# The last layer's gate and up products in seven block products instead of eight

## The chip, the cores and the metric

The kernel runs on one core of a Trainium2 chip. The metric is the device time of one execution in microseconds. Three executions of the kernel before took 2089.25, 2089.91 and 2090.18 us; the median, 2089.91 us, is what the changed kernel is held against.

## The reference

The model has two layers over 512 latent tokens (stream x) and 256 context tokens (stream c) of 1024 features. Each layer has a mixer part (pooling, windowed attention, spatial gating, three gated branches, an output projection) and then a feed-forward part. Only the feed-forward part of the second, last layer is changed:

```
def swiglu(h, w_in, w_out):
    gu = h @ w_in                                  # w_in [1024, 2 * 2816]
    return (silu(gu[..., :D_FF]) * gu[..., D_FF:]) @ w_out    # w_out [2816, 1024]

x = x + mod_x[5] * swiglu(modulate(x, norm2_gain, mod_x[3], mod_x[4]), w_ffn_in, w_ffn_out)
```

In the last layer it runs for the 512 latent tokens alone. h is the normed and modulated residual; gate is the first half of gu's columns, up is the second.

## The kernel before

**Layout.** Activations are feature-major: 128 features in the partitions, tokens along the columns; X holds the residual as 8 such tiles. A product of a weight block with the activations adds up 8 steps of 128 features in one PSUM bank.

**Split numbers.** Every large product is made of three matmuls in float32r: weights and activations are split into a high part (ScalarE copies with rounding, L272 for weights, L318 or L359 for activations) and an exact low part (VectorE subtracts, L273, L319, L360; a few on GpSimd). `gemm_step` (L289 to L292) then adds high x high, low x high and high x low. Each of these matmuls loads weights of its own.

**Weights.** `units` (L276) loads 4 KB a partition at a time from HBM into a raw tile (pool `rawp`, 4 buffers), by SyncE's queue (L284), and splits it into a `WH` and a `WL` tile (pool `hlp`, 3 buffers each). Activations, hidden tiles and the token-major result live in pool `act` (11 buffers of 8 KB a partition, tag S8).

**The feed-forward part** (`ffn`, L834). The 2816 hidden features are 22 tiles. For tile j, `half` (L873) makes the gate product of 128 features for 512 tokens (24 matmuls of 512 columns), then the up product; ScalarE takes silu of the gate out of PSUM (L883), VectorE multiplies by up (L886), and the result is split (L318, L319) into a hidden tile `fa`. After every fourth tile `chunk` (L847) makes the down products of the four tiles before: 8 feature tiles, 12 matmuls of 512 columns each, added to X by VectorE (L854). The first gate and up products of the last layer go by token halves (`first_halves`, L1036), since the second half of the tokens is normed while the first half's products run; `last_tiles` (L1015) does the same for the last output projections before it. The last two hidden tiles are multiplied with tokens in the partitions (`finish1`, L1071), into rows that `turn` (L1056) has transposed; the result is normed and stored there.

**The mixers' modulation sums.** `mod_steps` (L204) adds up weighted rows of w_mod on VectorE (L222), ScalarE and GpSimd (L220) beside the large products; its raw rows go through `rawp` too.

**What sets the order.** The lines give each instruction a priority. The framework's planner then runs the program in its own model of durations, gives each engine the ready instruction of the highest priority, and gives out tile buffers as they come free; that order is fixed in the program, and at run time each engine works through its own list and waits on semaphores.

Of the kernel before, what the change touches and what calls it, by code (L numbers as in the profile page):

```python
# [18 lines left out]
P = 128  # L19
# [16 lines left out]
class Stream:  # L36
    """Columns [t0, t0 + T) of the feature-major residual: the context or the latents."""
# [11 lines left out]
def hybrid_dit_kernel(ctx, tc, I, out):  # L49
# [4 lines left out]
    rawp = ctx.enter_context(tc.tile_pool(name="rawp", bufs=4))  # L54
    hlp = ctx.enter_context(tc.tile_pool(name="hlp", bufs=3))
# [37 lines left out]
    # rows of 128 features each, transposed to one column per row  # L93
# [50 lines left out]
    def to_features(s):  # L144
        """The stream's residual to feature-major, and its tokens' sums of squares."""
# [26 lines left out]
    def take_mod(l, t0, n, ps, nv):  # L172
        """Rows of 32 features each to columns: tiles t0 .. t0 + n of the layer's modulation vectors."""
# [11 lines left out]
    def mod_part(ps, h):  # L185
        """A quarter of the first layer's first shift and scale, on the tensor engine: loads, then two k-tiles at each step."""
# [17 lines left out]
    def mod_steps(l, u0, u1, stride=1):  # L204
        """The others, 512 at a time: weighted rows added up on the vector engines, then over the partitions."""
# [36 lines left out]
    class Filler:  # L242
        """Work that is interleaved, a step at a time, with the large products."""
# [24 lines left out]
    def split_unit(raw_ap, kt, n, nm, eng=None):  # L268
        """float32r high part and exact low part of a [P, kt, n] block of weights."""
# [6 lines left out]
    def units(src, kt, nm, engs=()):  # L276
        """src [kt*P, n] -> per n-tile (wh, wl) as [P, kt, 128] views, loaded 4 KB a partition at a time."""
# [54 lines left out]
    def token_ss(s, acc, nm):  # L332
        """Sums over the features of the squares that the tiles of acc hold."""
# [6 lines left out]
    def modulated(s, ss, A, Sh, nm, out, every=1, keep=False, HL=None):  # L340
        """Normed and modulated stream, split: the sums, the tokens' factors along the columns, the products."""
# [823 lines left out]
```

## Time and profile before

| | |
|---|---|
| median of 3 runs | 2089.91 us |
| the profiled execution, span | 2093.8 us |
| TensorE busy | 2024.5 us, 97% |
| VectorE, ScalarE, GpSimd busy | 1149.6, 744.4, 426.7 us |
| the last layer's gate, up and down products | about 1715.4 to 2073 us of the span |

The profile comes from one execution, which was 3.9 us longer than the median of the runs. Times in rows are us from the start of its span. Matmuls are pipelined: the time of one in a row overlaps the next one's, so the cost of a matmul in a long chain is the distance from one start to the next.

### The profile page before, as it was taken

How to read it: one execution, taken by the hardware profiler on the slowest of the kernel's cores; microseconds unless marked ns; L12 is line 12 of the kernel's file. 1: busy time of each engine (PE TensorE's matmuls, PEld its weight loads, DVE VectorE, ACT ScalarE, POOL GpSimd, SP SyncE). 2: the span in 40 equal slices, each digit the busy share in tenths (PEclk: the TensorE clock that was granted, in tenths of full speed). 3: DMA queues.
4: the chain of work that ended last, by engine and by line, in shares of the span. 5: the costliest groups of instructions: out<-in, count | busy, mean ns of one | idle time of the engine just before them, and what ended most of it. 6: DMA issues, size and time to landing. Idle time of an engine off the chain costs nothing.

```text
span 2093.8 us, 28850 instructions
## 1 busy us (share of the span) xinstructions
PE 2024.5 (97%) x11615; PEld 1715.0 (82%) x11615; DVE 1149.6 (55%) x1765; ACT 744.4 (36%) x1231; POOL 426.7 (20%) x358
## 2 busy tenths in 40 slices
PE   7998999999899999999999999999999999999998
PEld 6988988777677888888888888787778788888887
DVE  4878638675666653434334335765756664344335
ACT  3655434344333422121313124443422333222223
POOL 4426302023664411000102013301111130000000
PEclk9999999999999999999999999999999999999999
DMA  9755633231544232222323223423336643333331
GB/s 294 207 165 153 202 101 101 63 104 51 159 153 131 81 91 73 88 81 71 91 61 101 71 71 89 109 61 90 88 102 211 178 132 91 100 95 97 101 92 59
DMA packets 326181, 233.46 MB, mean 112 GB/s; under 512 B 7648, under 2 KB 299664, under 8 KB 326048
## 3 DMA queue, kind: packets, MB, share of 16 engines
q1 hardware_dynamic: 322528, 226.78, 36.1%
q0 software_dynamic: 3280, 4.76, 1.1%
q8 instruction: 91, 1.49, 0.3%
q14 instruction: 42, 0.34, 0.0%
q10 hardware_dynamic: 240, 0.08, 0.0%
HBM read 225.30 MB, written 2.10 MB: 109 GB/s over the span
## 4 chain that ended last, share of the span: by engine, by line
PE 81%; DVE 10%; DMA 3%; issue 2%; ACT 2%; POOL 2%; ACTq 0%; SPq 0%; POOLq 0%; DVEq 0%
PE pg1x L290 2%; PE pg1x L291 2%; PE pg1x L292 2%; PE pfg0x L292 2%; PE pfg0x L291 2%; PE pfg0x L290 2%; PE pfg1x L292 2%; PE pfo0x L290 2%; PE pfo0x L291 2%; PE pfu1x L291 2%; PE pfo0x L292 2%; PE pfu1x L292 2%; PE pfu1x L290 2%; PE pfg1x L290 2%; PE pfg1x L291 2%
## 5 line engine op out<-in xcount | busy, mean ns | idle before, releaser
L220 POOL TENSOR_TENSOR mac<-mac,mq 128x512 f32<-128x512 f32 x84 | 124.4, 1481 | 296.9 <-ACT mq L219 293.0
L273 DVE TENSOR_TENSOR wl_fu<-raw_fu,wh_fu 128x1024 fp32r<-128x1024 f32 x44 | 63.6, 1446 | 153.9 <-ACT wh_fu L272 153.8
L222 DVE SCALAR_TENSOR_TENSOR mac<-wm,scv,mac 128x512 f32<-128x512 f32 x140 | 131.0, 936 | 13.4 <-DMA wm<-in_w_mod_dram 10.6
L272 ACT ACTIVATE wh_fg<-raw_fg 128x1024 fp32r<-128x1024 f32 x44 | 46.6, 1059 | 181.1 <-PE pfo0x L292 65.7
L273 DVE TENSOR_TENSOR wl_fo<-raw_fo,wh_fo 128x1024 fp32r<-128x1024 f32 x42 | 54.7, 1303 | 69.3 <-ACT wh_fo L272 69.3
L272 ACT ACTIVATE wh_fo<-raw_fo 128x1024 fp32r<-128x1024 f32 x42 | 44.4, 1058 | 122.4 <-issue 120.2
L291 PE MATMUL pg0x<-n1x0h,wl_g0x 128*128 128x512 f32 x192 | 77.2, 402 | 8.9 <-DVE wl_g0x L273 8.9
L290 PE MATMUL pg0x<-n1x0h,wh_g0x 128*128 128x512 f32 x192 | 77.1, 402 | 1.5 <-ACT wh_g0x L272 1.5
L290 PE MATMUL pg1x<-n1x1h,wh_g1x 128*128 128x512 f32 x192 | 76.4, 398 | 0.0
L292 PE MATMUL pg0x<-n1x0l,wh_g0x 128*128 128x512 f32 x192 | 76.4, 398 | 0.0
L291 PE MATMUL pg1x<-n1x1h,wl_g1x 128*128 128x512 f32 x192 | 75.8, 395 | 0.0
L292 PE MATMUL pg1x<-n1x1l,wh_g1x 128*128 128x512 f32 x192 | 75.8, 395 | 0.0
L329 POOL TENSOR_TENSOR rs_fin<-v_fin,half_neg 128x1 f32<-128x1 f32 x4 | 2.9, 721 | 355.3 <-DVE v_fin L327 355.3
L290 PE MATMUL pfg1x<-n2x1h,wh_fg 128*128 128x512 f32 (+1 forms) x184 | 70.5, 383 | 0.8 <-ACT n2x1h L359 0.8
L854 DVE SCALAR_TENSOR_TENSOR X<-pfo0x,modv,X 128x512 f32<-128x512 f32 x48 | 36.0, 750 | 64.0 <-PE pfo0x L292 64.0
L292 PE MATMUL pfg1x<-n2x1l,wh_fg 128*128 128x512 f32 (+1 forms) x184 | 70.5, 383 | 0.5 <-POOL n2x1l L360 0.3
L290 PE MATMUL pfu1x<-n2x1h,wh_fu 128*128 128x512 f32 (+1 forms) x184 | 70.0, 380 | 0.0
L291 PE MATMUL pfu1x<-n2x1h,wl_fu 128*128 128x512 f32 (+1 forms) x184 | 70.0, 380 | 0.0
L291 PE MATMUL pfg1x<-n2x1h,wl_fg 128*128 128x512 f32 (+1 forms) x184 | 69.9, 380 | 0.0
L292 PE MATMUL pfu1x<-n2x1l,wh_fu 128*128 128x512 f32 (+1 forms) x184 | 69.9, 380 | 0.0
L290 PE MATMUL pfo0x<-fa,wh_fo 128*128 128x512 f32 x176 | 69.0, 392 | 0.0
L291 PE MATMUL pfo0x<-fa,wl_fo 128*128 128x512 f32 x176 | 69.0, 392 | 0.0
(708 smaller groups left out, 6540.1 us busy)
## 6 DMA issues: line engine op xcount, KB each, us to landing
wm<-in_w_mod_dram SPq DMA_DIRECT2D x96, 512.0 KB, 4.0
raw_fg<-in_w_ffn_in_dram SPq DMA_DIRECT2D x44, 512.0 KB, 3.9
raw_fu<-in_w_ffn_in_dram SPq DMA_DIRECT2D x44, 512.0 KB, 3.8
raw_fo<-in_w_ffn_out_dram SPq DMA_DIRECT2D x42, 512.0 KB, 3.4
raw_g0c<-in_w_in_dram SPq DMA_DIRECT2D x24, 512.0 KB, 3.9
raw_g0x<-in_w_in_dram SPq DMA_DIRECT2D x24, 512.0 KB, 4.2
raw_g1x<-in_w_in_dram SPq DMA_DIRECT2D x24, 512.0 KB, 3.9
raw_wo0c<-in_w_out_dram SPq DMA_DIRECT2D x8, 512.0 KB, 4.0
```

The lines of the kernel that those rows point to most:

```text
L220: G.tensor_tensor(a, a, q, ALU.add)
L222: V.scalar_tensor_tensor(a, raw[:, k, :], sck, a, ALU.mult, ALU.add)
L272: S.activation(wh, raw_ap, AF.Copy)
L273: (eng or V).tensor_tensor(wl, raw_ap, wh.bitcast(F32), ALU.subtract)
L290: T_.matmul(ps, wh, H, start=first, stop=False)
L291: T_.matmul(ps, wl, H, start=False, stop=False)
L292: T_.matmul(ps, wh, L, start=False, stop=last)
L329: G.tensor_tensor(rs, v, half_neg[:, :nb], ALU.pow)
L854: V.scalar_tensor_tensor(x, ps, modv[l][:, 40 + n, s.r:s.r + 1], x, ALU.mult, ALU.add)
```

## The change

The gate and up products of tile j are read as one 2 x 2 block product. The input features are halved (k tiles 0 to 3 and 4 to 7), the tokens are halved (columns 0 to 255 and 256 to 511), and the two rows of blocks are gate and up: A11, A12 are the two halves of the gate weights, A21, A22 those of the up weights; B11, B21 are the first tokens' feature halves, B12, B22 the second tokens'. Seven products of 4 k steps and 256 columns replace eight (Winograd's form of Strassen's scheme):

- weight sums on GpSimd: S1 = A21 + A22, S2 = S1 - A11, S3 = A11 - A21, S4 = A12 - S2;
- activation sums, once: T1 = B12 - B11, T2 = B22 - T1, T3 = B22 - B12, T4 = B21 - T2. B11, B21, T2, T1, T3, B22 and T4 are each split into high and low parts and kept in seven S8 tiles;
- products A11 B11, A12 B21, S2 T2, S1 T1, S3 T3, S4 B22, A22 T4. A bank P takes the products with B11, T2, T3 and T4 on top of each other, and its partial sums are read out in between; a bank R takes the ones with T1 and B22.

Each tile is four items (a: B11, B21; b: T2, T1; c: T3, B22; d: T4), each with a preparation (loads, sums, splits) and a run; down products are items too. `Pipeline` puts an item's preparation two items ahead of its run. The last layer's second norm keeps the normed tokens in float32 (`th0`, `th1`) and splits B11 and B21 as they come; `combine` makes the T's after the second token half. Tiles 0 to 2 run their item a first. `rawp` goes from 4 to 5 buffers and `hlp` from 3 to 4, for the whole kernel, and the scratch for GpSimd's DMA descriptors is set to 4096 bytes. The rows for the result and the load of final_gain are allocated at tile 21 instead of ahead of the feed-forward part. Comments are taken out.

```diff
-    rawp = ctx.enter_context(tc.tile_pool(name="rawp", bufs=4))
-    hlp = ctx.enter_context(tc.tile_pool(name="hlp", bufs=3))
+    rawp = ctx.enter_context(tc.tile_pool(name="rawp", bufs=5))
+    hlp = ctx.enter_context(tc.tile_pool(name="hlp", bufs=4))
...
+    class Pipeline:
+        def fill(self):
+            while len(self.ready) <= self.depth:
+                item = next(self.items, None)
+                if item is None:
+                    return
+                self.ready.append((item[1], item[0]()))
+        def step(self):
+            self.fill()
+            if not self.ready:
+                return False
+            do, w = self.ready.popleft()
+            do(w)
+            fill.tick()
+            return True
...
+        def split(self, nm, src, k0, k1, eng):
+            c = self.C[nm]
+            S.activation(c[:, 0, k0:k1, :], src, AF.Copy)
+            eng.tensor_tensor(c[:, 1, k0:k1, :], src, c[:, 0, k0:k1, :].bitcast(F32), ALU.subtract)
...
+        def norm(self, st, ss, i):
...
+            for k in range(KT):
+                V.tensor_tensor(t[:, k, :], X[:, k, st.cols], rb, ALU.mult)
+                a, b = A2[l][:, k, st.r:st.r + 1], modv[l][:, 24 + k, st.r:st.r + 1]
+                if k % 2:
+                    S.activation(t[:, k, :], t[:, k, :], AF.Identity, bias=b, scale=a)
+                else:
+                    V.tensor_scalar(t[:, k, :], t[:, k, :], a, b, ALU.mult, ALU.add)
+                if i == 0 and k % 2:
+                    nm = "B11" if k < 4 else "B21"
...
+                    self.split(nm, t[:, k - 1:k + 1, :], (k - 1) % 4, (k - 1) % 4 + 2, G if k % 4 == 1 else V)
+        def combine(self):
...
+            for h in (slice(0, 2), slice(2, 4)):
+                V.tensor_tensor(b11[:, h], b12[:, h], b11[:, h], ALU.subtract)
+                V.tensor_tensor(T2[:, h], b22[:, h], b11[:, h], ALU.subtract)
+                self.split("T2", T2[:, h], h.start, h.stop, V)
+            self.split("T1", b11, 0, 4, G)
+            V.tensor_tensor(b12, b22, b12, ALU.subtract)
+            self.split("T3", b12, 0, 4, V)
+            self.split("B22", b22, 0, 4, G)
+            V.tensor_tensor(b21, b21, T2, ALU.subtract)
+            self.split("T4", b21, 0, 4, V)
+        def product(self, ps, w, k0, nm, first):
+            c = self.C[nm]
+            wh, wl = w
+            for k in range(4):
+                H, L = c[:, 0, k, :], c[:, 1, k, :]
+                T_.matmul(ps, wh[:, k0 + k, :], H, start=first and k == 0, stop=False, skip_group_check=True)
+                T_.matmul(ps, wl[:, k0 + k, :], H, start=False, stop=False, skip_group_check=True)
+                T_.matmul(ps, wh[:, k0 + k, :], L, start=False, stop=k == 3, skip_group_check=True)
...
+            def sums():
...
+                s1, s2, s3, s4 = (att.tile([P, 4, P], F32, tag="pr", bufs=4, name=f"S{x}{j}") for x in (1, 2, 3, 4))
+                G.tensor_tensor(s1, a21, a22, ALU.add)
+                G.tensor_tensor(s2, s1, a11, ALU.subtract)
+                G.tensor_tensor(s3, a11, a21, ALU.subtract)
+                G.tensor_tensor(s4, a12, s2, ALU.subtract)
...
+            def run_a(w):
+                d["P"] = ps_y.tile(...)[:, :256] if early == "y" else pmain(f"pP{j}")[:, :256]
+                self.product(d["P"], w, 0, "B11", True)
+                S.activation(d["m"][:, 0:256], d["P"], AF.Copy)
+                ps = pmain(f"pS{j}")[:, :256]
+                self.product(ps, w, 4, "B21", True)
+                V.tensor_tensor(d["g_"][:, 0:256], ps, d["m"][:, 0:256], ALU.add)
+                S.activation(d["g_"][:, 0:256], d["g_"][:, 0:256], AF.Silu)
+            def run_b(w):
+                self.product(d["P"], w, 0, "T2", False)
+                S.activation(d["m"][:, 256:512], d["P"], AF.Copy)
+                d["R"] = pmain(f"pR{j}")[:, :256]
+                self.product(d["R"], w, 4, "T1", True)
+                S.activation(d["m5"], d["R"], AF.Copy)
+            def run_c(w):
+                self.product(d["P"], w, 0, "T3", False)
+                V.tensor_tensor(d["h"][:, 256:512], d["P"], d["m5"], ALU.add)
+                self.product(d["R"], w, 4, "B22", False)
+                V.tensor_tensor(d["g_"][:, 256:512], d["R"], d["m"][:, 256:512], ALU.add)
+                S.activation(d["g_"][:, 256:512], d["g_"][:, 256:512], AF.Silu)
+            def run_d(w):
+                self.product(d["P"], w, 0, "T4", False)
+                V.tensor_tensor(d["h"][:, 0:256], d["P"], d["g_"][:, 0:256], ALU.mult)
+                G.tensor_tensor(d["h"][:, 256:512], d["h"][:, 256:512], d["g_"][:, 256:512], ALU.mult)
+                split_act(*A(), d["h"])
...
-    mixer(SX, 1, *hs["x"], ..., mid=context_keys, last=last_tiles)
-    ffn([SX], 1, hs, finish1, parts=first_halves, ahead=..., turn=turn)
+    tail.extend(ffn_seven(seven, SX, 1, finish1, turn_out))
+    mixer(SX, 1, *hs["x"], ..., mid=context_keys, last=last_tiles)
+    run(norms[1])
+    seven.combine()
+    tail[1]()
...
-    nc = bacc.Bacc("TRN2", target_bir_lowering=False, num_devices=1)
+    nc = bacc.Bacc("TRN2", target_bir_lowering=False, num_devices=1, dynamic_dma_scratch_size=4096)
```

The weights' preparation of a tile splits 1024 columns for item a (A11, A12), 512 each for S2, S1, S3 and S4, and 512 for A22. `ffn_seven` holds the down products of four tiles as four items of two feature tiles each, as before after every fourth tile, into banks of pool `ps_s`.

## Rows read from the trace of the kernel before

**Rows 1.** Page, part 1: engine, busy us, share of the span, instructions.

```profile
PE 2024.5 (97%) x11615; PEld 1715.0 (82%) x11615; DVE 1149.6 (55%) x1765; ACT 744.4 (36%) x1231; POOL 426.7 (20%) x358
```

**Rows 2.** Page, part 4: the chain that ended last, share by engine.

```profile
PE 81%; DVE 10%; DMA 3%; issue 2%; ACT 2%; POOL 2%; ACTq 0%; SPq 0%; POOLq 0%; DVEq 0%
```

**Rows 3.** Busy time by stretch; the first line names the columns.

```profile
core 0: us, PE busy (x) PEld busy (x) DVE busy (x) ACT busy (x) POOL busy (x), PEclk, DMA share, GB/s
...
110.00:235.00 125.00, 116.44 (x964) 111.53 (x963) 97.99 (x154) 67.02 (x117) 57.45 (x52) 0.99 0.59 174
...
345.00:500.00 155.00, 152.03 (x954) 119.85 (x952) 107.19 (x235) 70.22 (x150) 30.88 (x32) 1.00 0.27 77
500.00:660.00 160.00, 143.25 (x695) 112.52 (x695) 102.71 (x107) 59.66 (x84) 91.22 (x56) 0.95 0.46 139
...
1500.00:1660.00 160.00, 159.21 (x812) 126.61 (x812) 100.67 (x154) 50.22 (x76) 28.72 (x24) 1.00 0.49 151
...
1715.40:1732.50 17.10, 15.77 (x125) 14.30 (x124) 13.89 (x35) 13.14 (x28) 7.72 (x10) 1.00 0.32 93
1732.50:2073.00 340.50, 340.49 (x1517) 282.10 (x1516) 137.35 (x149) 90.27 (x109) 0.00 (x0) 1.00 0.31 92
```

**Rows 4.** PE timeline (start us, us): two starts 24 matmuls apart, for each width.

```profile
1702.06 0.28 PE L292 MATMUL po1x<-yo1x,wh_wo1x 128*128 128x256 f32 x1
...
1704.94 0.28 PE L292 MATMUL po1x<-yo1x,wh_wo1x 128*128 128x256 f32 x1
...
1803.23 0.39 PE L290 MATMUL pfu1x<-n2x1h,wh_fu 128*128 128x512 f32 x1
...
1808.67 0.39 PE L290 MATMUL pfg1x<-n2x1h,wh_fg 128*128 128x512 f32 x1
```

**Rows 5.** Groups by line, DVE, 1732.5 to 2073: busy us, mean ns, idle before.

```profile
L854 DVE SCALAR_TENSOR_TENSOR X<-pfo1x,modv,X 128x512 f32<-128x512 f32 x40 | 30.0, 750 | 44.1 <-PE pfo1x L292 44.1
...
L273 DVE TENSOR_TENSOR wl_fg<-raw_fg,wh_fg 128x1024 fp32r<-128x1024 f32 x20 | 24.5, 1225 | 7.4 <-ACT wh_fg L272 7.4
...
L319 DVE TENSOR_TENSOR fa<-sg1x,fa 128x512 fp32r<-128x512 f32 x21 | 14.4, 685 | 0.0
```

**Rows 6.** Groups by line, ACT, from 1690 on.

```profile
L272 ACT ACTIVATE wh_fg<-raw_fg 128x1024 fp32r<-128x1024 f32 x22 | 23.3, 1060 | 78.9 <-PE pfo1x L292 39.4 <-issue 19.6 <-PE pfu1x L292 19.4
...
L318 ACT ACTIVATE fa<-sg1x 128x512 fp32r<-128x512 f32 x22 | 13.5, 616 | 2.4 <-DVE sg1x L886 2.4
...
L359 ACT ACTIVATE n2x1h<-t_n2x 128x256 fp32r<-128x256 f32 x16 | 6.3, 412 | 2.3 <-DVE t_n2x L358 2.0
```

**Rows 7.** Groups by line, POOL, whole span.

```profile
L372 POOL TENSOR_TENSOR sq_m1x<-sq_m1x,sq_m1x 128x512 f32<-128x512 f32 x4 | 7.1, 1763 | 21.8 <-ACT sq_m1x L368 21.8
...
L717 POOL TENSOR_TENSOR ws0x<-a0x 128x527 f32<-128x527 f32 x4 | 4.3, 1066 | 36.6 <-issue 21.9 <-ACT a0x L711 14.7
```

**Rows 8.** Groups by line, DVE: 1715 to 1732.5, then the whole span.

```profile
L354 DVE TENSOR_TENSOR t_n2x<-X,ps_rb_n2x 128x256 f32<-128x256 f32 x15 | 5.7, 408 | 1.0 <-PE ps_rb_n2x L346 1.0
...
L273 DVE TENSOR_TENSOR wl_g0x<-raw_g0x,wh_g0x 128x1024 fp32r<-128x1024 f32 x24 | 38.1, 1586 | 37.4 <-ACT wh_g0x L272 37.3
```

**Rows 9.** Timeline at the start of the feed-forward part.

```profile
1715.88 0.39 PE L290 MATMUL pfg1x<-n2x1h,wh_fg 128*128 128x256 f32 x1
...
1723.88 0.75 DVE L354 TENSOR_TENSOR t_n2x<-X,ps_rb_n2x 128x256 f32<-128x256 f32 x2 [0.99 <-PE ps_rb_n2x L346]
...
1730.62 0.53 DVE L360 TENSOR_TENSOR n2x1l<-t_n2x,n2x1h 128x256 fp32r<-128x256 f32 x1 [0.48 <-ACT n2x1h L359]
```

**Rows 10.** What PE waited for, whole span: us in total, times, longest.

```profile
PE pg0x L291 <- DVE wl_g0x L273: 8.9, 3, 4.8
...
PE pb0x L291 <- DVE wl_b0x L273: 5.6, 2, 4.7
```

**Rows 11.** The longest such wait's end: SP's load, and PE's stretch after.

```profile
550.64 0.37 SPq L284 DMA_DIRECT2D raw_g0x<-in_w_in_dram  x1
...
562.00:566.00 4.00, 3.90 (x9) 3.13 (x10) 0.65 (x2) 0.00 (x0) 3.69 (x3) 0.50 0.67 207
```

More of the change, by code (lines that the diff above doesn't have):

```diff
@@ L1 @@
 import math
+from collections import deque
 from contextlib import ExitStack
@@ L941, in ffn, with __init__ @@
         chunk(heads[-1])
+    class Pipeline:
+        def __init__(self, items, depth):
+            self.items, self.depth, self.ready = iter(items), depth, deque()
+        def fill(self):
[12 more added lines that the diff above has]
+            return True
@@ L1011, in hybrid_dit_kernel @@
     norms = []
-    us_first = []
-    ahead = up_units(1, 0, FCH * P)
+    seven = Seven(1)
+    tail = []
     def last_tiles(one, acc):
-        hs["x"] = pair_tiles(KT, SEQ, "n2x1")
         for i, st in enumerate(halves):
@@ L1020, in last_tiles @@
             part = [acc[0][:, c]]
-            norms.append(modulated(st, partial(token_ss, st, part, f"n2x1{i}"), A2[1], modv[1][:, 24:32, :], f"n2x1{i}", [],
-                                   HL=[[y[:, c] for y in x] for x in hs["x"]]))
+            norms.append(seven.norm(st, partial(token_ss, st, part, f"n2x1{i}"), i))
             for n in range(KT - 3, KT):
@@ L1026, in last_tiles, with turn_out @@
                 if i and n == KT - 3:
[L1027 removed]
+                    steps(norms[0], 1)
                 elif i and n == KT - 2:
+                    steps(norms[0], 2)
+                    tail[0].fill()
+                elif i:
                     steps(norms[0], 1)
[L1030 to L1033 removed]
         run(norms[0])
[L1036 to L1053 removed]
+    late = {}
     ssf = cst.tile([P, 4, 2], F32, name="ssf")
[L1056 removed]
+    def turn_out(i):
         if i == 0:
+            late["yt"] = [act.tile([P, 2, D], F32, tag="S8", name=f"yt{x}") for x in range(2)]
+            rows = act.tile([P, 2, D], F32, tag="S8", name="rows")
+            fg, mrow = late["rows"] = rows[:, 0, :], rows[:, 1, :]
+            nc.gpsimd.dma_start(fg, I["final_gain"].unsqueeze(0).to_broadcast([P, D]))
             ps = ps_s.tile([P, 1024], F32, tag="ps", name="ps_mrow")
@@ L1062, in turn @@
             S.activation(mrow, ps, AF.Copy)
+        yt = late["yt"]
         for b in range(2):
@@ L1073, in finish1 @@
         ws = []
+        yt = late["yt"]
+        fg, mrow = late["rows"]
         for c in range(2):
@@ L1116, in finish1 @@
         store(3)
-    ffn([SX], 1, hs, finish1, parts=first_halves, ahead=[chain([w], us) for w, us in zip(us_first, ahead)], turn=turn)
+    tail.extend(ffn_seven(seven, SX, 1, finish1, turn_out))
+    mixer(SX, 1, *hs["x"], mods=mod_steps(1, 4, 10), end=lambda: fill.add(mod_steps(1, 10, 12)), mid=context_keys, last=last_tiles)
+    run(norms[1])
+    seven.combine()
+    tail[1]()
 _INS = ["x", "c", "ctx", "c_ctx", "w_mod", "b_mod", "norm1_gain", "norm2_gain", "w_in", "w_pool", "pool_scale",
```

142 lines of the change are left out of this document (121 added, 21 removed).

## The prediction

> **What bounds the kernel now.** I read the page's busy shares first, then the chain, then the busy times by stretch, then the starts of single matmuls. TensorE is busy 97% of the span, VectorE 55% [rows 1], and the chain that ended last lies on PE for 81% and on DVE for 10% [rows 2]. The stretches say where that holds: from 1732.5 to 2073, where the last layer's gate, up and down products run, PE is busy 340.49 of 340.5 us while DVE is busy 137 and ACT 90 and POOL nothing [rows 3]. There nothing but the number and width of the matmuls sets the time. It does not hold everywhere: from 500 to 660 PE loses 16.75 of 160 us, and from 1715.4 to 1732.5, the entry of the changed part, it is short of inputs too [rows 3]. So the change has four places to be priced: the products themselves, their entry, the new load on the other engines beside them, and, because two buffer pools grow for the whole kernel, the mixers ahead of them.
>
> **The products.** In the chain, 24 matmuls of 512 columns take 1808.67 - 1803.23 = 5.44 us, 0.2267 each, and 24 of 256 columns 1704.94 - 1702.06 = 2.88 us, 0.120 each [rows 4]. Half the columns is thus not half the time: 2 x 0.120 is 0.0133 us above 0.2267. Both rows have new weights for each matmul, so the price of loading weights twice as often per column is in them.
> Before, a tile takes 48 matmuls of 512 columns, 10.88 us; the first tile goes by token halves, 96 of 256, 11.52 us. All 22: 21 x 10.88 + 11.52 = 240.0 us. After, a tile takes 7 products x 4 steps x 3 = 84 matmuls of 256 columns, 10.08 us; all 22: 221.8 us. The change removes 18.2 us of TensorE time: 12.5% of the columns, but 7.6% of the time.
> The Trainium skill ("TensorE: Matmul & The Clock Gate", Back-to-back issue gap) gives a matmul N columns over 2.4 GHz plus about 2.5 ns, so 0.216 and 0.109 us. By that the tile would go from 10.36 to 9.17 us and the saving would be some 26 us; the two rows are 0.011 us above it at either width, and since there are more matmuls after than before, that difference speaks against the change. The rows decide.
>
> **The entry.** T2 can't be made before the second token half is normed, while item a needs the first half alone. Before, the factors of the second half reach DVE at 1723.88 and its last low part is cut at 1730.62, with PE waiting in between [rows 9]. From 1715.4 to 1732.5 PE had 96 x 0.120 = 11.5 us of product and some 2 us of small matmuls (norm sums, factors, w_mod sums), so about 3.6 of 17.1 us were lost. After, counted from the same 1723.88: DVE has 8 multiplications by the factors (0.408 each [rows 8]) and 4 scalings of the same width (taken as 0.408), 4.9 us; then, at 512 columns and 0.685 each [rows 5], two subtractions for T1, two for T2 and two low parts of T2, 4.1 us, with one ACT copy of 0.616 [rows 6] not covered. T2 is ready near 1733.5. Items a of tiles 0 to 2 need only B11 and B21; they are 72 x 0.120 = 8.6 us from 1715.88 on, with the small matmuls and the read-outs between their second products until about 1726.5. So PE runs dry for some 7 us. Then DVE still has T3, T4, their low parts (4 x 1.225 [rows 5]) and the low weights of items c and d of tile 0 (3 x 0.685): T4's product of tile 0 ends near 1742, by when PE has done 17.3 us of products and 2 us of small work of 26.5. The loss is about 7.5 us for 3.6 before: 4 us more. And a gap of that length costs more behind it: after PE's wait that ended at 562, the granted clock is 0.50 for 562 to 566, the level of 1.2 GHz [rows 11]; some 5 us at half speed are worth about 2.5 us. I take 6 us for the entry. Lower bound 0, if the planner fills the gap with later items' first products; upper bound 11, if DVE runs beside POOL at the rate of rows 8 (1586 against 1225 ns [rows 5], so 14 us of DVE work become 18).
>
> **The other engines beside the products.** For a tile with its share of down products PE now has 10.08 + 5.44 = 15.5 us. DVE: 1.225 + 5 x 0.685 for the low weights, 0.685 for the low hidden tile, 1.225 for the low down weights, 2 x 0.750 for X [rows 5], and four read-outs of 256 columns at 0.408 [rows 8]: 9.7 us, 62%, where it was 40% [rows 3]. ACT: 2 x 1.060, 6 x 0.616, five read-outs or silus at 0.412 [rows 6]: 7.9 us, 51%. POOL, idle before: 4 sums of 512 columns, 1.07 us each when undisturbed and 1.76 when not [rows 7], and one product of 256: 5 to 8 us, 32 to 50%. SP's queue has the same loads. No engine passes PE, so by load the cover holds. What is new is that PE itself waits: bank P is read out three times within a tile, each time behind a product of 1.44 us into another bank, which must cover a semaphore, an ACT or DVE queue that may be inside an operation of 1.06 to 1.23 us, and the read-out of 0.41. The planner has other work to put there (down products, the next tile's item a), but by its own durations. The trace has no such stage; the nearest ones by load are four [rows 3]: 1500 to 1660 (DVE 63%, ACT 31%, POOL 18%), where PE is idle 0.5%; 345 to 500 (69, 45, 20), 1.9%; 110 to 235 (78, 54, 46), 6.8%; 500 to 660 (64, 37, 57), 10.5%. I take 345 to 500, nearest in DVE and ACT: 2% of 331 us (221.8 + 5 x 96 x 0.2267) is 6.5 us. Bounds: 1.7 and 35 us.
>
> **The end.** Behind the last tile's d stand a multiplication of 256 columns, a copy and a subtraction of 512, 0.41 + 0.62 + 0.69 us. Before, the rows' transposes covered the same chain; now they come one item earlier, but the final products of the hidden tile before (9 matmuls of 512 columns in three banks, 2.0 us) need only that one. Cost 0; if that cover is gone, 2 us.
>
> **The mixers.** One more raw tile and one more pair of split tiles let a load and a split run one unit further ahead. From 500 to 660 PE's waits for low weights are 8.9 and 5.6 us [rows 10]; for the longest, the raw weights were asked for only at 550.64 and PE resumed at 562 at half clock [rows 11]. The granted clock of 0.95 over those 160 us [rows 3] is another 8 us. All of it together is 22 us, the most to be had. But the low weights also queue behind w_mod sums on DVE, and the planner's new order may open waits of its own; the trace bounds that loss by nothing, and I allow 5 us. I take a gain of 8 us, a bit over a third. The smaller scratch for GpSimd's descriptors is shown by no row; its few transfers in the mixers may wait a little, 0 to 3 us, taken as 0.
>
> **The sum.** -18.2 + 6 + 6.5 - 8 = -13.7 us. On the profiled execution's 2093.8 us that is 2080.1; its span stands 3.9 us above the median of the runs, so 2076 in runs.
>
> **The rivals.**
> 1. The buffers matter more than the products: the waits from 500 to 660 go, and the planner covers the read-outs as from 1500 to 1660: -18.2 + 6 + 1.7 - 22 = -32.5, so 2057. For it: the late load in rows 11. Against it: the DVE queue.
> 2. The gain is eaten: entry 11, read-outs 3% (10 us), mixers unchanged: +3, so 2086 to 2094 with small differences. For it: every one of PE's new waits has a cover of only 1.44 us.
> 3. Slower: DVE and POOL disturb each other through the whole stretch, run behind the planner's order, and PE waits as from 500 to 660, 10.5%: -18.2 + 6 + 35 - 5 = +18, so 2108. It decides from 7% of idle PE on (24 us). For it: POOL goes from 0 to 32 to 50% here, and both engines' rows are half again as long in company [rows 5, 7, 8]. Against it: 1500 to 1660, with the same DVE load, and that the waits from 500 to 660 stand behind long runs of w_mod sums, which this stretch has none of. The Trainium skill ("SBUF — State Buffer", Who interferes with whom) calls the port that the two share an exclusive lock; if each subtraction and each sum waited its turn, that would be this rival.
> 4. That the products get no shorter, since loading weights might set the pace at 256 columns: excluded by the 0.120 us of rows 4.
>
> **Chances.** Forecast 0.57, rival 1 0.14, rival 2 0.14, rival 3 0.15. About 0.2%, 4.2 us, is what a measurement can tell: faster is below 2085.7, slower above 2094.1. The forecast and rival 1 lie below: faster 0.71, same 0.14, slower 0.15. The range 2058 to 2096 leaves out most of rival 3 and half of rival 1.
>
> **What would show it.** Starts 0.120 us apart in the seven products; 84 of them a tile; a gap of some 7 us in PE near 1726 with half clock behind it; PE's idle share from there to the end near 2%, with waits on the read-outs; DVE near 62% and POOL near 40%; in the mixers fewer waits for low weights. The prediction is wrong if PE's idle share there is above 5%, if the entry costs nothing, or if the mixers move by more than 15 us.

## The result, and the profile after

The changed kernel took 2145.24 us in the median of four runs (2140.53 to 2148.37), the kernel before 2090.05 in the same session: a ratio of 1.0259, 95% interval 1.0242 to 1.0276. It is 55 us slower, where 14 us faster was forecast, and it lies above the whole range.

The page's busy times by engine, after (as [rows 1]):

```profile
PE 2031.1 (95%) x12359; PEld 1751.9 (82%) x12359; DVE 1264.9 (59%) x1923; ACT 807.9 (38%) x1401; POOL 591.6 (28%) x464
```

The busy times by stretch: first those of [rows 3], then the entry (up to the first down product) and the rest of the last feed-forward part.

```profile
core 0: us, PE busy (x) PEld busy (x) DVE busy (x) ACT busy (x) POOL busy (x), PEclk, DMA share, GB/s
110.00:235.00 125.00, 112.62 (x905) 106.21 (x905) 93.12 (x153) 64.75 (x119) 55.32 (x49) 0.96 0.53 159
345.00:500.00 155.00, 153.39 (x937) 122.36 (x936) 112.23 (x234) 72.06 (x150) 30.14 (x32) 1.00 0.28 80
500.00:660.00 160.00, 149.16 (x767) 117.17 (x766) 108.75 (x122) 63.30 (x96) 96.49 (x60) 0.97 0.47 141
1500.00:1660.00 160.00, 156.43 (x817) 123.59 (x816) 93.25 (x146) 49.66 (x76) 30.96 (x26) 1.00 0.46 142
1726.10:1800.40 74.30, 60.07 (x431) 57.24 (x429) 61.28 (x86) 40.04 (x74) 41.21 (x25) 0.86 0.24 72
1800.40:2127.00 326.60, 302.08 (x1970) 275.28 (x1969) 207.53 (x255) 128.67 (x230) 123.38 (x87) 0.96 0.28 83
```

Before, the last stretch of [rows 3] had PE busy 340.49 of 340.5 us at clock 1.00 and POOL empty. Now PE idles 14.2 of the entry's 74.3 us and 24.5 of the next 326.6, at clocks of 0.86 and 0.96, with POOL busy 38% beside it. The products themselves are as short as forecast: in the timeline of TensorE (start, us), two starts 24 matmuls apart are 1840.49 - 1837.62 = 2.87 us, 0.120 each, as in [rows 4].

```profile
1837.62 0.28 PE L1038 MATMUL pP<-cbT,wh_su 128*128 128x256 f32 x1
...
1840.49 0.28 PE L1038 MATMUL pS<-cbB,wh_sg 128*128 128x256 f32 x1
```

To say where the 52.8 us between the two profiled executions (2093.8 and 2146.6) lie, I took the distance from each matmul's start to the next, took off 0.120 or 0.2267 us, and called what is left over lost: waits, half-clock matmuls, small matmuls between. The marks are the end of the last output projection (po1x), the first down product (pfo1x) and the first of the final products.

| part | before | after | difference |
|---|---|---|---|
| up to the last po1x | 1715.4 | 1726.1 | +10.7 |
| pure products of the last feed-forward part | 348.6 | 330.1 | -18.5 |
| lost in its entry | 5.5 | 25.4 | +19.9 |
| lost from there to the final products | 4.8 | 45.1 | +40.3 |
| the whole of that part, mark to mark | 359.2 | 401.0 | +41.8 |
| behind it | 19.2 | 19.5 | +0.3 |

(The parts of the feed-forward part fall 0.3 to 0.4 us short of the marks, at the stretches' edges. Of the 4.8 and 45.1 us, 4.4 and 5.1 are the transposes of the result's rows ahead of the final products.) What TensorE waited for from 1726 on, after (us in total, times, longest):

```profile
PE pfo1x L291 <- DVE X L1146: 17.7, 5, 4.1
PE pP L1038 <- ACT m L1104: 10.9, 11, 2.6
PE pP L1038 <- ACT cbT L984: 4.8, 1, 4.8
PE pP L1039 <- DVE wl_sc L1070: 2.7, 1, 2.7
```

The first comes back at every chunk of down products; the second is the read-out of bank P, 3 times in the entry and 8 times behind it, between the chunks (6.8 us there). One wait of the first kind, in the timeline of all engines (loads of weights and the matmuls between left out):

```profile
1871.06 1.29 POOL L1057 TENSOR_TENSOR S<-raw_u 128x512 f32<-128x512 f32 x1 [8.58 <-DVE gt L1115]
...
1871.67 1.77 DVE L274 TENSOR_TENSOR wl_fo<-raw_fo,wh_fo 128x1024 fp32r<-128x1024 f32 x1 [0.72 <-ACT wh_fo L273]
...
1872.43 2.16 POOL L1058 TENSOR_TENSOR S<-S,raw_g 128x512 f32<-128x512 f32 x1
...
1873.69 1.98 DVE L274 TENSOR_TENSOR wl_fo<-raw_fo,wh_fo 128x1024 fp32r<-128x1024 f32 x1
1874.56 2.27 POOL L1059 TENSOR_TENSOR S<-raw_g,raw_u 128x512 f32<-128x512 f32 x1
1876.79 1.28 POOL L1060 TENSOR_TENSOR S<-raw_g,S 128x512 f32<-128x512 f32 x1
...
1878.03 0.72 POOL L1121 TENSOR_TENSOR h<-h,gt 128x256 f32<-128x256 f32 x1
1878.78 0.63 ACT L319 ACTIVATE fa<-h 128x512 fp32r<-128x512 f32 x1 [5.31 <-POOL h L1121]
...
1879.44 0.69 DVE L320 TENSOR_TENSOR fa<-h,fa 128x512 fp32r<-128x512 f32 x1 [3.77 <-ACT fa L319]
1880.05 1.40 DVE L1146 SCALAR_TENSOR_TENSOR X<-pfo1x,modv,X 128x512 f32<-128x512 f32 x2
1880.94 0.77 PE L291 MATMUL pfo1x<-fa,wh_fo 128*128 128x512 f32 x1 [3.38 <-DVE X L1146]
1881.50 0.63 PE L292 MATMUL pfo1x<-fa,wl_fo 128*128 128x512 f32 x1
```

Read it backwards. PE waits 3.38 us for a bank that X's update (L1146) must empty. VectorE does X late, because its list has the low part of the hidden tile (L320) ahead of it; that waits for ScalarE's copy, and that for the h product on GpSimd (L1121), which stands behind the next tile's four weight sums. The sums themselves take 1.28 to 2.27 us; the VectorE subtraction of 1024 columns beside them takes 1.77 and 1.98 us, 1.225 before [rows 5]. By these rows the two engines take turns: the sum that starts at 1872.43 ends 1.15 us after the end of the subtraction beside it (1871.67 + 1.77 = 1873.44), the next subtraction ends 1.08 us after the end of that sum (1874.59), the next sum 1.16 us after that subtraction's (1875.67). Each thus lasts about its own time behind the other's end. It is the same over the whole stretch from 1800.4 on: when the rest of the other engine's running operation is taken off, the 66 VectorE subtractions that overlap a GpSimd operation take 0.54 to 0.69 us (512 columns) or 1.08 to 1.23 (1024), where undisturbed ones take 0.68 to 0.69 and 1.21 to 1.23. Behind the gap the matmuls are 0.43 us apart: from 1881 to 1886 the granted clock is 0.50, the level of 1.2 GHz, after the wait of 3.38 us. So two causes are mixed here, a queue (h behind the sums) and a mutual slowing of GpSimd and VectorE. And a third place, the pools, moved the mixers. The experiments take them apart.

### The profile page after: what moved, and what is told of

Read it like the earlier page. It is cut to its first block, busy times and chain, and to the rows that moved or that the text cites. A ratio compares the mean times of both kernels' runs of the same rounds, so it can differ in the third digit from the quotient of the medians.

```text
span 2146.6 us, 30872 instructions
## 1 busy us (share of the span) xinstructions
PE 2031.1 (95%) x12359; PEld 1751.9 (82%) x12359; DVE 1264.9 (59%) x1923; ACT 807.9 (38%) x1401; POOL 591.6 (28%) x464
## 5 line engine op out<-in xcount | busy, mean ns | idle before, releaser
L291 PE MATMUL pfo1x<-fa,wh_fo 128*128 128x512 f32 x160 | 67.1, 419 | 17.7 <-DVE X L1146 17.7
L274 DVE TENSOR_TENSOR wl_fg<-raw_fg,wh_fg 128x1024 fp32r<-128x1024 f32 x22 | 34.5, 1567 | 64.4 <-ACT wh_fg L273 64.3
L1057 POOL TENSOR_TENSOR S<-raw_u 128x512 f32<-128x512 f32 x22 | 32.0, 1453 | 142.6 <-DVE wl_sb L1070 97.9
L291 PE MATMUL pfg0x<-n2x0h,wh_fg 128*128 128x512 f32 x176 | 68.9, 391 | 0.4 <-ACT n2x0h L360 0.4
L293 PE MATMUL pfg0x<-n2x0l,wh_fg 128*128 128x512 f32 x176 | 68.9, 391 | 0.2 <-DVE n2x0l L361 0.2
L291 PE MATMUL pfo0x<-fa,wh_fo 128*128 128x512 f32 x176 | 69.0, 392 | 0.0
L292 PE MATMUL pfg0x<-n2x0h,wl_fg 128*128 128x512 f32 x176 | 68.7, 391 | 0.0
L293 PE MATMUL pfo0x<-fa,wh_fo 128*128 128x512 f32 x176 | 68.6, 390 | 0.0
L291 PE MATMUL pfu0x<-n2x0h,wh_fu 128*128 128x512 f32 x176 | 68.5, 389 | 0.0
L292 PE MATMUL pfu0x<-n2x0h,wl_fu 128*128 128x512 f32 x176 | 68.5, 389 | 0.0
L293 PE MATMUL pfu0x<-n2x0l,wh_fu 128*128 128x512 f32 x176 | 68.5, 389 | 0.0
```

What stands on the lines that cost most here:

```text
L274: (eng or V).tensor_tensor(wl, raw_ap, wh.bitcast(F32), ALU.subtract)
L291: T_.matmul(ps, wh, H, start=first, stop=False)
L292: T_.matmul(ps, wl, H, start=False, stop=False)
L293: T_.matmul(ps, wh, L, start=False, stop=last)
L1057: G.tensor_tensor(s1, a21, a22, ALU.add)
```

## The experiments

Each was timed against the kernel before, which had a median of 2089.95 to 2091.35 us in the sessions.

**The pools alone, in the kernel before.**

```diff
-    rawp = ctx.enter_context(tc.tile_pool(name="rawp", bufs=4))
-    hlp = ctx.enter_context(tc.tile_pool(name="hlp", bufs=3))
+    rawp = ctx.enter_context(tc.tile_pool(name="rawp", bufs=5))
+    hlp = ctx.enter_context(tc.tile_pool(name="hlp", bufs=4))
...
-    nc = bacc.Bacc("TRN2", target_bir_lowering=False, num_devices=1)
+    nc = bacc.Bacc("TRN2", target_bir_lowering=False, num_devices=1, dynamic_dma_scratch_size=4096)
```

> The kernel before with the pool sizes of the change alone (five raw tiles, four pairs of split tiles, the smaller scratch). Up to the start of the last feed-forward part the changed kernel is 10.8 us later than the one before (last output projection at 1726.3 for 1715.5). Theory A, the pools reorder the mixers and that costs: about 2101 us, with PE's waits on score read-outs near 90 to 135 and on tanh read-outs in the gates. Theory B, the mixers are later because the planner works around the new part: 2090 us, no change. My prediction's own term, the pools help by 8: 2082 us.

2098.75 us, ratio 1.0039 (1.0024 to 1.0054). The pools cost, where I had them gain 8 us. What TensorE waited for over the span of this run:

```profile
PE pt0c L536 <- DVE pr0c L522: 7.3, 4, 4.4
...
PE s1x L505 <- ACT pr1x L518: 3.1, 1, 3.1
...
PE pg0x L291 <- DVE wl_g0x L273: 0.2, 1, 0.2
```

The wait for low weights of [rows 10], 8.9 us, is gone, as forecast. But the context's attention now waits 7.3 us for VectorE's normalised probabilities, 2.4 before, and the context's mixer ends 10 us later (261.3 to 271.4). The changed kernel shows the same two lines, 7.2 and 0.4 us. These two nearly cancel: the last down product of layer 0's latent tokens ends at 1258.2 us here, at 1260.8 before and at 1258.6 in the run with the smaller descriptor space alone (below). What is left of the loss is in layer 1's mixer, 459.5 us long here for 454.5 before, where one wait in the attention (s1x) grew from 0.2 to 3.1 us.

**The h product on VectorE.**

```diff
-                G.tensor_tensor(d["h"][:, 256:512], d["h"][:, 256:512], d["g_"][:, 256:512], ALU.mult)
+                V.tensor_tensor(d["h"][:, 256:512], d["h"][:, 256:512], d["g_"][:, 256:512], ALU.mult)
```

> The changed kernel with one line moved: the product of silu(gate) and up for the second 256 tokens on VectorE instead of GpSimd. Theory Q (queues): that product stands behind four weight sums on GpSimd, the hidden tile's split behind it, the updates of X behind that on VectorE, both banks of the down products stay full and PE waits 3.4 us and falls to half clock, five times: 18 us of waits and 9 us of clock go, about 2120 us. Theory P (VectorE and GpSimd slow each other by the shared port, whatever the order): the waits move elsewhere, 2140 us or more.

2129.58 us, ratio 1.0187 (1.0170 to 1.0203): 16 us back, by taking the product out of GpSimd's queue. The loss behind the entry falls from 45.1 to 30.8 us; the rest stays.

**Both banks of each ps_s tile for the down products.**

```diff
+                    pair = ps_s.tile([P, 1024], F32, tag="ps", name=f"pfo{l}{s.name}{c0}{n}")
                     for i in range(2):
-                        ps = ps_s.tile([P, 1024], F32, tag="ps", name=f"pfo{l}{s.name}{c0}{n + i}")[:, :512]
+                        ps = pair[:, i * 512:(i + 1) * 512]
```

> The changed kernel with both banks of each down-product tile used: four banks for the down products instead of two, nothing else. Theory Q: PE may run four feature tiles ahead of VectorE, 10.9 us instead of 5.4, so a delay of 3.4 us is covered: the 18 us of waits and the 9 us of clock behind them go, about 2120 us. Theory P: VectorE is late for good, the waits come back within the chunk: 2140 us or more.

2149.82 us, ratio 1.0284 (1.0269 to 1.0300). No gain, and the wait on X grows:

```profile
PE pfo1x L291 <- DVE X L1147: 23.9, 5, 5.3
```

By the code a pair of banks is freed only when both its feature tiles are added to X, which may be why the wait grew; no run takes that apart. What is late is VectorE, not the number of banks; the queue theory's forecast for this run fell.

**No weight sums.**

```diff
-                G.tensor_tensor(s1, a21, a22, ALU.add)
-                G.tensor_tensor(s2, s1, a11, ALU.subtract)
-                G.tensor_tensor(s3, a11, a21, ALU.subtract)
-                G.tensor_tensor(s4, a12, s2, ALU.subtract)
-                d["S"] = s1, s2, s3, s4
+                d["S"] = a21, a22, a11, a12
```

> The changed kernel without the four weight sums on GpSimd: the blocks themselves are split in their place, so the output is not the reference's. Theory Q: GpSimd's queue is empty, the product for the second tokens comes at once: as with that line moved, about 2115 us, and the start of the part gains some 5 us as its factors no longer wait behind sums, 2110 us. Theory P: VectorE runs undisturbed too, all of the stretch's 30 us of waits and 10 us of clock go and most of the start's loss: below 2100 us.

2097.47 us, ratio 1.0036 (1.0024 to 1.0049): 48 us less than the change. Behind the entry 6.4 us are lost of 45.1, and 5.1 of those are the rows' transposes. The profile shows no wait of TensorE there at all. So nearly the whole loss hangs on the four sums; the 84 matmuls, the read-outs of bank P and the seven combinations cost TensorE some 1.3 us there, and the h product, which is on GpSimd in this run too, costs nothing without the sums ahead of it.

**The sums and the product on VectorE, with the large and with the old pools.**

```diff
-                G.tensor_tensor(s1, a21, a22, ALU.add)
-                G.tensor_tensor(s2, s1, a11, ALU.subtract)
...
+                V.tensor_tensor(s1, a21, a22, ALU.add)
+                V.tensor_tensor(s2, s1, a11, ALU.subtract)
...
```

> The four weight sums (L1057 to L1060) and the h product (L1121) move from GpSimd to VectorE; nothing is left out. VectorE has then some 4 x 0.69 + 0.41 = 3.2 us more per tile of 14.8 us, and no two-input work of GpSimd beside it. Theory G (what hurts is GpSimd: its sums slow VectorE's parts, and the product queues behind them): the steady part comes back to within 5 us of the run without sums, 2097 to 2108 us. Rival L (the work itself is too much, wherever it is done: VectorE at some 85 % becomes late for the residual update and for the low parts): 2120 us or more, with TensorE waits on VectorE in every tile.

> As the run before it, with the old pools besides (rawp 4, hlp 3, the default descriptor space). Theory A (the larger pools cost the mixers 8 us, as in the kernel before with larger pools, and the sevens need none of them): 6 to 10 us below the run with the large pools. Rival B (the sevens need the fourth weight buffer, since each product now has half the columns and a weight pair lasts 10 us / 3.5): the gain in the mixers is paid back in the last layer, the same time within 3 us or more, with TensorE waits on weight parts in the steady part.

2100.14 us (ratio 1.0045, 1.0031 to 1.0060) and 2099.77 (1.0041, 1.0026 to 1.0056). The same work on the engine that is the busier one costs TensorE next to nothing behind the entry: the stretch 1800 to 2040 has PE busy 239.62 of 240 us with VectorE at 74% and GpSimd empty. Theory L fell. (The low parts of T1 and B22, in the entry, are still GpSimd's in both runs.)

```profile
1800.00:2040.00 240.00, 239.62 (x1680) 224.97 (x1679) 177.83 (x291) 111.81 (x203) 0.59 (x1) 1.00 0.34 101
```

With the old pools the mixers end 7.7 us earlier (1715.1 for 1722.8), the feed-forward part takes 5.7 longer (362.7 for 357.0), 4.8 of it in the entry, and the end behind it 2.0 longer (21.6 for 19.6): rival B in effect, though its place is the entry and not the steady part.

**Operations of GpSimd that nobody waits for.** First as copies of the sums without loads to wait for, with the h product on VectorE and on GpSimd:

```diff
+                va, vb = vtm[:, 0:4, :], vtm[:, 2:6, :]
-                G.tensor_tensor(s1, a21, a22, ALU.add)
+                G.tensor_tensor(s1, va, vb, ALU.add)
...
-                d["S"] = s1, s2, s3, s4
+                d["S"] = a21, a22, a11, a12
```

> Four GpSimd operations of the same kind and size per tile, but on tiles that nobody waits for; the weight blocks are used without sums (so what is computed is not the scheme's result), and the h product is on VectorE. What is left of GpSimd is only its presence beside VectorE. Theory P (sharing slows VectorE's parts from 0.69 to 1.4 to 1.8 us, and that makes the residual updates late): near the run with only the h product moved, 2115 to 2132 us. Theory Q (only who waits for GpSimd matters: the weight parts for the sums, the h product behind them): 2095 to 2101 us, as without sums.

> As the run before it, the h product on GpSimd again, so that it stands in GpSimd's queue behind the four operations. Theory Q: the queue gives back most of the loss, 2110 to 2125 us, while the run before it is at 2098. Theory P: the run before it has most of the loss and this one 10 to 18 us more, as the h product was worth in the changed kernel (2145 against 2130).

2153.74 and 2150.84 us (ratios 1.0303, 1.0286 to 1.0321, and 1.0286, 1.0271 to 1.0302). They answer another question than I put. The planner drew all 88 operations forward into layer 1's mixer, where their operand was ready from 1526 on, and the last layer ran without them (355.5 and 354.9 us). Two stretches of that mixer in the first of the two runs:

```profile
1560.00:1620.00 60.00, 46.95 (x210) 37.09 (x208) 50.20 (x37) 9.47 (x11) 59.30 (x36) 0.93 0.50 151
1620.00:1680.00 60.00, 36.90 (x128) 28.37 (x129) 22.98 (x21) 7.75 (x10) 51.84 (x39) 0.73 0.26 76
```

GpSimd is full, the mixer's own GpSimd operations stand behind the copies, and PE loses 36 of 120 us. For theories P and Q they are void; in the next run the operations are tied to the loads.

```diff
                 G.tensor_tensor(s4, a12, s2, ALU.subtract)
-                d["S"] = s1, s2, s3, s4
+                d["S"] = a21, a22, a11, a12
...
-                G.tensor_tensor(d["h"][:, 256:512], d["h"][:, 256:512], d["g_"][:, 256:512], ALU.mult)
+                V.tensor_tensor(d["h"][:, 256:512], d["h"][:, 256:512], d["g_"][:, 256:512], ALU.mult)
```

> The two runs with sums of other tiles had them in the wrong place: the planner drew operations without loads to wait for forward into the mixer. Here the four weight sums are made by GpSimd of the loaded blocks, as in the change, but nobody reads them (the parts are made of the weight blocks themselves, so what is computed is not the scheme's result), and the h product is on VectorE. Theory P (GpSimd beside VectorE slows VectorE's parts and updates, and that alone makes TensorE wait): near the run with only the h product moved, 2115 to 2132 us, with TensorE waits on VectorE. Theory Q (the loss comes by those that wait for the sums): as without sums, 2095 to 2101 us.

2128.52 us, ratio 1.0176 (1.0161 to 1.0191). Nobody reads a sum, and 31 of the 48 us are there: theory P. By the marks of the table above, 21 of the 31 lie behind the entry, 3 in it and 7 ahead of it; there the first tiles' sums also stand ahead of a small step of the norm in GpSimd's queue, for which TensorE waits 2.9 us. The groups of VectorE from 1840 to 2060 (busy us, mean ns, idle before) tell how, first in the change, then in this run, then with the sums on VectorE:

```profile
L1070 DVE TENSOR_TENSOR wl_sc<-S,wh_sc 128x512 fp32r<-128x512 f32 x26 | 26.0, 1011 | 1.4 <-ACT wh_sc L1069 1.0
...
L274 DVE TENSOR_TENSOR wl_fo<-raw_fo,wh_fo 128x1024 fp32r<-128x1024 f32 x12 | 18.7, 1559 | 9.7 <-ACT wh_fo L273 9.7
L1146 DVE SCALAR_TENSOR_TENSOR X<-pfo1x,modv,X 128x512 f32<-128x512 f32 x24 | 17.7, 749 | 31.7 <-PE pfo1x L293 31.7
L320 DVE TENSOR_TENSOR fa<-h,fa 128x512 fp32r<-128x512 f32 x13 | 16.6, 1275 | 11.3 <-ACT fa L319 11.3
L1070 DVE TENSOR_TENSOR wl_su<-raw_u,wh_su 128x512 fp32r<-128x512 f32 x13 | 16.5, 1272 | 0.0
```

```profile
L274 DVE TENSOR_TENSOR wl_fo<-raw_fo,wh_fo 128x1024 fp32r<-128x1024 f32 x12 | 19.1, 1595 | 9.7 <-ACT wh_fo L273 9.7
L1146 DVE SCALAR_TENSOR_TENSOR X<-pfo1x,modv,X 128x512 f32<-128x512 f32 x24 | 17.7, 747 | 27.2 <-PE pfo1x L293 27.2
L320 DVE TENSOR_TENSOR fa<-h,fa 128x512 fp32r<-128x512 f32 x14 | 12.8, 913 | 0.0
```

```profile
L1146 DVE SCALAR_TENSOR_TENSOR X<-pfo1x,modv,X 128x512 f32<-128x512 f32 x30 | 22.5, 749 | 20.6 <-PE pfo1x L293 20.6
L274 DVE TENSOR_TENSOR wl_fo<-raw_fo,wh_fo 128x1024 fp32r<-128x1024 f32 x16 | 19.5, 1221 | 10.1 <-ACT wh_fo L273 10.1
...
L320 DVE TENSOR_TENSOR fa<-h,fa 128x512 fp32r<-128x512 f32 x14 | 9.6, 684 | 0.0
```

With both inputs in SBUF an operation stretches from 684 to 913 or 1275 ns, from 1221 to 1559 or 1595. X's update, which has one input in PSUM, takes 749, 747 and 749: it does not stretch, nor do the 8 of its 40 operations that overlap one of GpSimd's in the changed kernel (0.75 us each). So the loss behind the entry splits by the runs' traces: 20.8 us by the mutual slowing (27.2 lost with unread sums and h on VectorE, less 6.4 without sums), 3.6 by the parts that wait for the sums (30.8 with the sums read, h on VectorE), and 14.3 by the h product's place behind the sums (45.1). The place, since the same product on GpSimd without sums costs nothing (6.4 us lost); the steps are differences between runs whose order the planner may have changed elsewhere too.

**Another entry: tiles 0 and 1 as eight products.** Gate and up of tiles 0 and 1 go by token halves with B11, B21, then B12, B22; the T's are made meanwhile on VectorE, T2, T1, T3 and T4 behind the four `then` items.

```diff
+            yield g0, lambda w: h0("g", 0)
+            yield u0, lambda w: h0("u", 0)
+            yield g1, lambda w: h1("g", 0)
+            yield lambda: None, then(h0, ("g", 1))
+            yield lambda: None, then(h0, ("u", 1))
+            yield lambda: None, then(h1, ("g", 1))
+            yield u1, then(h1, ("u", 0), ("u", 1))
+            for j in range(2, NF):
```

> Sums and h product on VectorE, old pools, and another entry: hidden tiles 0 and 1 go as eight plain products by token halves, which need no second half and no T; the T's are made beside them, on VectorE, and tiles 2 to 21 go as seven. The sevens then save 20/22 of 18.6 us = 16.9. The run with old pools lost 24 us at the entry (72.7 us for 48.8 of products); theory N (what was missing is work for TensorE that needs no T): some 5 us of loss stay, 2099.8 - 19 + 1.7 = 2082 us, 2077 to 2087. Rival S (VectorE with some 11 us of sums and parts, or the 11 tiles of 8 KB, are late all the same): the loss moves to the first product with T2, 2090 us or more.

> As the run before it with the larger pools (rawp 5, hlp 4, descriptor space 4096). The mixers end some 7.7 us later with them; with the small pools the entry of the sevens was 5 us longer, which the plain tiles no longer need. Theory A: 5 to 9 us above the run with the old pools. Rival B (the fourth weight buffer is needed at the plain tiles too, whose parts are held for both halves): the same within 3 us.

2082.04 us with the old pools, ratio 0.9955 (0.9938 to 0.9971): faster than both kernels, at theory N's number. The entry loses 7.3 us (59.0 for 51.7 of products), 23.9 with the T's in the way (72.7 for 48.8). Two things changed in it, the plain tiles and the low parts of T1 and B22, which left GpSimd; no run tells the two apart. From 17 us into the entry on, the stretch 1726.1 to 1800 has PE busy 73.37 of 73.9 us, at clock 1.00:

```profile
1726.10:1800.00 73.90, 73.37 (x520) 68.78 (x519) 59.42 (x89) 37.34 (x62) 0.00 (x0) 1.00 0.32 93
```

With the large pools 2090.35 us, 0.9995 (0.9985 to 1.0004): 8 us more, theory A.

**Which of the pools.** The first line below alone, then with the second, then with the third.

```diff
+    nc = bacc.Bacc("TRN2", target_bir_lowering=False, num_devices=1, dynamic_dma_scratch_size=4096)
...
+    rawp = ctx.enter_context(tc.tile_pool(name="rawp", bufs=5))
...
+    hlp = ctx.enter_context(tc.tile_pool(name="hlp", bufs=4))
```

> The kernel before with the descriptor space of 4096 alone, pools as they were. With larger pools and this space it took 2098.75. Theory D (the space is what costs, by GpSimd's transfers): 2096 to 2100 us. Theory A (the buffers are what costs, by another order of the planner): 2088 to 2092 us.

> The kernel before with the descriptor space of 4096 and rawp at 5 buffers; hlp stays at 3. Both larger pools together took 2098.75 us, the space alone 2090.56. Theory R (a fifth raw buffer lets the sums of w_mod and later loads run further ahead and shares the transfers otherwise, which delays the first mixer's weights): 2096 to 2100 us. Theory H (not this one): 2088 to 2092 us.

> The kernel before with the descriptor space of 4096 and hlp at 4 buffers; rawp stays at 4. Theory H (a fourth weight buffer lets ScalarE and VectorE split weights earlier than what the mixer itself waits for, which costs more than it gives): 2096 to 2100 us. Theory R: 2088 to 2092 us, or less, since low weights are what the mixers wait for most.

The space alone: 2090.56 us (0.9999, 0.9989 to 1.0008). The fifth raw buffer: 2075.70 (0.9930, 0.9915 to 0.9945). The fourth weight buffer: 2092.47 (1.0004, 0.9994 to 1.0013). Neither costs anything measurable alone; theories R and H both fell. The raw buffer alone gives 15 us: the wait of [rows 10] for pg0x's low weights shrinks from 8.9 to 1.2 us, and the context's attention does not pay for it (mixer's end at 262.4 us, 261.3 before).

```profile
PE pb0x L291 <- DVE wl_b0x L273: 4.3, 2, 3.5
...
PE pg0x L291 <- DVE wl_g0x L273: 1.2, 1, 1.2
```

The fourth weight buffer alone brings part of the attention's waits (4.6 us, the context's mixer's end at 265.8), both together 7.3 us. The longer mixer of layer 1 comes with both only: 459.5 us, with the raw buffer alone 451.1, with the weight buffer alone 453.0, with the descriptor space alone 452.9. That the planner lets splits of weights go ahead of the softmax on VectorE is my reading and was not taken apart.

**All that helped.** The plain entry, sums and product on VectorE, hlp 3, and five or six raw buffers.

> The sevens with plain tiles 0 and 1, sums and h product on VectorE (2082.04 us with the old pools), now with the fifth raw buffer and the 4096 descriptor space, hlp at 3. Theory R (the fifth raw buffer frees the latent mixer of layer 0 of its waits for low weights, whatever the last layer does): the kernel before gained 15 us by it, so 2067 us, 2063 to 2071. Rival O (the planner's order of the mixers depends on all that follows, and the gain belongs to that one program): 2078 us or more.

> As the run before it with six raw buffers. Theory R2 (one more removes the waits that five leave: 4.3 us at the third branch's low weights in layer 0's latent mixer): 2 to 5 us below five. Rival F (five are enough, and a sixth only lets later loads go ahead of earlier needs): the same or up to 8 us more.

2069.51 us (0.9896, 0.9881 to 0.9910) and 2067.52 (0.9889, 0.9871 to 0.9907): the raw buffer's gain carries over, 12.5 of 15 us. A sixth is 2 us better in the median, with runs that overlap; it is not settled. The feed-forward part takes 348.9 us with five, 359.2 before, and behind its entry TensorE is full:

```profile
1756.70:2046.00 289.30, 289.29 (x1967) 268.22 (x1966) 214.68 (x340) 129.43 (x230) 0.59 (x1) 1.00 0.32 95
```

Seven products are worth 6 us here against the kernel before with the raw buffer alone (2075.70, in another session), where the feed-forward part alone gained 10 (348.9 for 359.2); the rest went into mixers that end later (1698.6 for 1694.6).

## Why the prediction was wrong

**The products: right.** -18.2 forecast, -18.5 found, at 0.120 and 0.2267 us apiece. By the spacing that the Trainium skill ("TensorE: Matmul & The Clock Gate", Back-to-back issue gap) gives for a matmul by itself, the saving would have been an estimated 26 us; the trace is with the rows.

**The other engines beside the products: this step failed, and it decides.** It read "The trace has no such stage; the nearest ones by load are four" and "I take 345 to 500, nearest in DVE and ACT: 2% of 331 us ... is 6.5 us". The runs found 40.3. The loads were forecast well (VectorE 62%, found 60% undisturbed, 172.51 of 288 us in the run without sums, and with the waiting for GpSimd 207.53 of 326.6, 64%; GpSimd about 40%, found 38%). So was what the term was named for: without the sums, that stretch loses 1.6 us more than in the kernel before (6.4 for 4.8). The choice of the stage was wrong: 345 to 500 has POOL at 20%. Nearest in POOL were 110 to 235 at 46% and 500 to 660 at 57%, with 6.8 and 10.5% of PE idle [rows 3]; that the 7.5% found lies between them proves little, since the waits there are of other kinds. The rows for this were on the page: both engines' operations are half again as long in company [rows 5, 7, 8]. I used those for a bound, not for the sum. What the runs show in its place: 38.7 of the 45.1 us lost hang on GpSimd's sums (6.4 are left without them), 20.8 by the turns that the two engines take and 14.3 by h's place in the queue. That is rival 3, its mechanism and its place, though the queue of h behind the sums, a third of the loss, was in no rival. With 7.5% of PE idle it lay just above rival 3's own point of decision; nearly half of the 45.1 us lost, though, is not idle time but half-clock and small matmuls, which that point left out.

The Trainium skill ("SBUF — State Buffer", Who interferes with whom) has the shared port as an exclusive lock, and names VectorE operations with two SBUF inputs as those that it meets. The trace agrees in both: X's update stays at 749 ns, and the subtractions beside GpSimd last their own time and the rest of the operation that runs there; behind the entry the longest of 512 columns takes 1.785 us, its own 0.684 and less than one undisturbed sum of 1.29. The rule stood in the prediction behind rival 3, and should have stood behind the sum.

**The entry: right in mechanism, mis-sized.** +6 forecast, +19.9 found, above the upper bound of 11. The gap came (4.79 us at 1736.4, 7 forecast), but it was not the only one: T1's low part took GpSimd 5.75 us and B22's 3.32 (1024 columns, 1.225 on VectorE before [rows 5]), and there a low part of the weights was late too (wl_sc, 2.7 us of PE's waits). The engine timelines at the gap:

```profile
1741.19 0.58 PE L1038 MATMUL pP<-cbT,wh_sb 128*128 128x256 f32 x1 [4.79 <-ACT cbT L984]
...
1742.16 5.75 POOL L985 TENSOR_TENSOR cbT<-th,cbT 128x1024 fp32r<-128x1024 f32 x1 [5.61 <-ACT cbT L984]
...
1744.47 1.21 DVE L985 TENSOR_TENSOR cbT<-th,cbT 128x1024 fp32r<-128x1024 f32 x1
...
1745.94 3.05 DVE L985 TENSOR_TENSOR cbT<-th,cbT 128x1024 fp32r<-128x1024 f32 x1
...
1747.87 3.32 POOL L985 TENSOR_TENSOR cbB<-th,cbB 128x1024 fp32r<-128x1024 f32 x1
```

The low parts of T1 and B22 stood in no term of the working; GpSimd's company stood only in the bound. Two of its sums were short besides: the eleven products up to T4's of tile 0 make 15.8 us, not 17.3, and VectorE's work as listed is 16 us, not 14. Even without the weight sums 19.3 us stay lost in the entry (67.9 for 48.6): T2 must wait for the second half (a gap of 3.7 us there), and the two low parts on GpSimd hold wl_sc up as before (2.7 us). Plain tiles, with those low parts off GpSimd, took this to 7.3.

**The mixers: the named mechanism right, the sign of the sum wrong.** -8 forecast, +10.7 found. The waits for low weights went as forecast (8.9 to 0.4 us), and the latent mixer of layer 0 made up some 10 us by it; but the context's mixer before it had ended nearly 12 us later, so that layer 0's part for the latent tokens ended only 1.2 us later in all (1260.8 us before). The rest of the loss came behind it: layer 1's mixer ran 464.1 us for 454.5. "The planner's new order may open waits of its own" was allowed 5 us; it took more than all that was won. The fifth raw buffer by itself gives 15 us, more than the guess; with the fourth weight buffer beside it that gain was gone.

**The end** cost 0.3 us, as priced (0, with 2 us as the bound).

## What to carry to other kernels

Before work is given to an idle engine, look whether it shares something with the busy one: here GpSimd's sums, idle capacity by the profile's page, cost 48 us (39 of them behind the entry), and the same sums on VectorE, at 74%, at most some 3 us (2100.14 for 2097.47). When a new stage is priced by the nearest old one, take the nearest in the pair that disturbs, not in the mean load. Change pools one at a time: one buffer, of no effect on the time by itself, took away the 15 us of the other.

## What was not expected of the hardware

Two-input VectorE subtractions from SBUF of 512 columns went from a mean of 684 ns to 1275 beside GpSimd's sums, whose time went from 1.29 to as much as 2.27 us, while an operation with a PSUM input stayed at 749 ns. A low part of 1024 columns took GpSimd 5.75 us: it ends 2.23 us after the last of four VectorE subtractions that followed one another (1744.47 + 1.21 = 1745.68), so by the times it was let in only then. VectorE's next subtraction took 3.05 us for its own 1.22 and ends 1.08 after it, and GpSimd's next low part 3.32, ending 2.20 after that. And operations without a reader or a wait are not free in a planned kernel: 88 of them, made for tiles that run from 1713 on, were drawn forward to 1526 and put the end of the mixer off by some 50 us (1776.4 for 1722.8 with the sums on VectorE).
